# A fourth Strassen unit in the last gate pair of a decoder trunk layer

## The chip, the cores and the metric

One core of one Trainium2 chip. The metric is the device time of one execution in microseconds, the median over several runs. Engines are called PE or TensorE (matmul), PEld (its weight load), DVE or VectorE, ACT or ScalarE, POOL or GpSimd, and SP (SyncE, which issues the DMAs).

## The reference

One layer on 256 tokens of 2048 features, all in float32. A combined projection feeds a short convolution and a gated recurrence, two merge gates join them, `w_o` projects back into the residual, and then comes the part that this case is about:

```python
x = x + m @ w_o[i]
gate = jax.nn.sigmoid(rmsnorm(x, ple_norm_g[i]) @ w_ple_gate[i])     # 256 x 2048 by 2048 x 2048
x = x + gate * (p[i] @ w_ple_proj[i])
return rmsnorm(x, final_norm_g)
```

## The kernel before

**Tiling.** The tokens are two tiles of 128 (`t` = 0, 1). Weight columns come in groups of `CW` = 512, weight rows in chunks of 256 (two contractions of 128). A float32 product is made as three matmuls of 128 x 128 by 128 x 512: every operand is split into a high part (ScalarE, line 166, tiles `whi`, `xh`) and the rest (VectorE, line 167, `wlo`, `xl`), and high by high, high by rest and rest by high are summed in PSUM. So each weight tile goes from DRAM into `raw` (three buffers of 1 MB, filled from SP's queue, lines 119 to 131), is split, and is used. VectorE reads `raw` last, so its split is what lets the third load after it start.

**Strassen units.** Where two column groups share the left operand, a chunk can be done for both groups at once as a 2 x 2 by 2 x 2 block product (token tiles by contractions, contractions by groups). Plainly that is 8 block products; in Winograd's form of Strassen's scheme, 7. A unit costs vector work instead: the left operand's four sums (`forms`, lines 787 to 795, tiles `So0` and `So1` for the last pair), and four sums of the weights (`combine_weights`, lines 184, 187 and 188, made in place in `raw` and in a tile `t2`). Seven weight blocks of 128 x 512 are then split, as three tiles of 128 x 1024 and one of 128 x 512; a plain chunk of both groups has four, in two tiles of 128 x 1024. A program such as

```python
LATE = (0, 4), ("S", 0), (0, 6), ("S", 1), (2, 3), ("S", 2), (1, 4), (1, 6)
```

sets the order of a pair: `("S", c)` is a unit on chunk c; `(u, c)` with u = 0 or 1 is chunks c and c + 1 of group u alone; `(2, c)` is chunk c of both groups, plainly. Each entry is one load of 1 MB. The products of an entry are made in `pair_products` (line 1293), those of a plain group in `product` (line 1269).

**Banks.** PSUM has four banks under the tag `g` and four under `s`. A pair holds its four results (t, group) in `g` and the four products that several results share (numbers 1, 5, 6 and 7) in `s`. When they are complete, `sums` joins them: ScalarE copies product 1 out of its bank (line 868), and VectorE adds the others step by step (line 855). A tag's banks are given out in turn, so the next one asked for waits for the oldest to be read.

**The last 75 us.** First group 0 of `w_ple_gate`, plain. Then groups 1 and 2 as a pair by `LATE`. Then group 3 (`last_group`) in three passes over the same eight weight steps: all 512 columns for t = 0, then 256 and 256 for t = 1. Behind each finished gate half stand a sigmoid (ScalarE, line 1025), the product with the projection (VectorE, 1028), the sum into the residual `xs` (VectorE, 1029), its squares (ScalarE, 1030) and the gain (GpSimd, 1037). For the last group these are lines 1045, 1046, 1049 and 1053; lines 1062 to 1074 sum the squares, and the output is scaled (1087 to 1091) and stored.

**Order.** The program is written in the order of the weight steps; splits are issued some steps ahead of their products, and the rest of the vector work is written between them. Each engine then runs its own list in order, and waits on semaphores.

Of the kernel before, what the change touches and what calls it, by code (L numbers as in the profile page):

```python
# [23 lines left out]
CW = 512  # L24
# [19 lines left out]
INNER = (0, 4), ("S", 0), (0, 6), ("S", 1), (2, 3), ("S", 2), (1, 4), (1, 6)  # L44
FRONT = (0, 2), (0, 4), (0, 6), ("S", 0), (1, 2), ("S", 1), (1, 4), (1, 6)
OUT = (0, 4), ("S", 0), (1, 4), ("S", 1), (2, 3), ("S", 2), (0, 6), (1, 6)
LATE = (0, 4), ("S", 0), (0, 6), ("S", 1), (2, 3), ("S", 2), (1, 4), (1, 6)


PRM_GMIX, PRM_GPLE, PRM_GHG, PRM_LB, PRM_CONV = 0, 16, 32, 40, 48  # L50
# [5 lines left out]
def hybrid_kernel(ctx, tc, xT, x, pT, prm, gfin, masks, w_in, w_a, w_b, w_o, w_pg, w_pp, out):  # L56
# [28 lines left out]
    def nm(s):  # L85
        uid[0] += 1
        return f"{s}_{uid[0]}"
# [5 lines left out]
    def bank(tag):  # L93
        return ps.tile([P, CW], F32, tag=tag, bufs=4, name=nm(tag))
# [48 lines left out]
    def split(pos, c0=0, c1=2 * CW):  # L143
        part = part_of[pos]
        src = load(pos)[:, part % 2, :]
        if joint[pos]:

            src = load(pos)[:, part == 3, :]
            if part == 1:
                src, c1 = half[unit_of[pos]], CW  # L150

        pool, n = (pools["late"], 6) if (pos - state.get("late", len(steps))) % 10 < 6 and "late" in state else (wp, 4)
        places = [(pool, n, tag) for tag in ("whi", "wlo")]
        n = len(MORE[more(pos)])
        if pos % (4 + n) < n:
            places = [(pools[name], 1 + (tag == "X"), tag) for name, tag in MORE[more(pos)][pos % (4 + n)]]
        if pos not in parts:
            parts[pos] = tuple(
                pool.tile([P, 2 * CW << (tag[:3] == "yaT")], F32R, tag=tag, bufs=n, name=nm("w" + x))[:, : 2 * CW] for (pool, n, tag), x in zip(places, ("hi", "lo"))
            )  # L160
        hi, lo = parts[pos]
        s = slice(c0, c1)
        with ExitStack() as order:
            for i in (*(state["splits"] if more(pos) == "inner" or any(pos in at for at in tied) else ()),):
                order.enter_context(tc.issue_after(i))
            a = nc.scalar.activation(out=hi[:, s], in_=src[:, s], func=AF.Copy)  # L166
            v = nc.vector.tensor_tensor(  # L167
                out=lo[:, s], in0=src[:, s], in1=hi[:, s].bitcast(F32), op=ALU.subtract
            )
        state["splits"] = (a.ins, v.ins)  # L170
        if joint[pos] and part == 0:
            combine_weights(pos)
# [31 lines left out]
    groups += [("OO", 0, w_o, 0, "mT", OUT), ("O", 2, w_o, 2, "mT"), ("O", 3, w_o, 3, "mT")]  # L204
    groups += [("PG", 0, w_pg, 0, "x1T"), ("GP", 1, w_pg, 1, "x1T", LATE), ("PG", 3, w_pg, 3, "x1T")]
    steps = []
# [744 lines left out]
    def ep_o(j, psum):  # L951
# [18 lines left out]
        if j < 2:  # L970
# [6 lines left out]
            yield  # L977
            chunks = [c for u, c in LATE if u == "S" and c // 2 == j]
            r = x1.rearrange("p (u k t) -> p u k t", u=2, k=2)[:, : len(chunks)]
# [59 lines left out]
    def last_half(t, h, psum):  # L1039

        xs, pw, ss, n = state["x"], state["pw", 3], state["ss3"], CW // 2
        gt = t4()
        squares, gt = gt[:, : n + (t == 1 and h == 1)], gt[:, :n]
        d = xs[:, t, 3 * CW + h * n : 3 * CW + (h + 1) * n]
        nc.scalar.activation(out=gt, in_=psum, func=AF.Sigmoid, scale=state["rstd2"][:, t : t + 1])
        nc.vector.tensor_tensor(  # L1046
            out=gt, in0=gt, in1=pw[:, t * CW + h * n : t * CW + (h + 1) * n], op=ALU.mult
        )
        nc.vector.tensor_tensor(out=d, in0=d, in1=gt, op=ALU.add)
        if t == 1 and h == 1:  # L1050

            d = state["whole"][:, NT * D - n : NT * D + 1]
        nc.vector.scalar_tensor_tensor(
            out=squares, in0=d, scalar=1.0 / D, in1=d, op0=ALU.mult, op1=ALU.mult,
            accum_out=ss[:, t * 6 + 3 + h : t * 6 + 4 + h],
        )

    def sums_so_far(t):

        tot = state["tot3", t] = sc(1, "tot3", 2)  # L1060
        ss = state["ss3"]
        nc.vector.tensor_tensor(
            out=ss[:, t * 6 + 3 : t * 6 + 4], in0=ss[:, t * 6 + 3 : t * 6 + 4],
            in1=ss[:, t * 6 + 5 : t * 6 + 6], op=ALU.add,
        )
        nc.vector.tensor_reduce(
            out=tot, in_=ss[:, t * 6 : t * 6 + 4], axis=mybir.AxisListType.X, op=ALU.add
        )
        if t == 1:

            root = sc(1, "tot3", 2)
            nc.vector.tensor_scalar(out=tot, in0=tot, scalar1=float(D), scalar2=None, op0=ALU.mult)
            nc.gpsimd.tensor_tensor(out=root, in0=tot, in1=mhalf[:, :1], op=ALU.pow)
            nc.vector.tensor_tensor(out=state["more"], in0=tot, in1=root, op=ALU.mult)
# [29 lines left out]
    def ep_last(t, halves):  # L1104

        last_half(t, 0, halves[0])
        sums_so_far(t)
        last_half(t, 1, halves[1])
        last_norm(t)
        yield  # L1110
# [138 lines left out]
    def advance():  # L1249
        for e in list(active):  # L1250
            step(e)
# [12 lines left out]
    def product(psum, op, k, t, hi, lo, first, last, which=(0, 1, 2)):  # L1264

        oh, ol = (x[:, k, t * P : (t + 1) * P] for x in op)
        for n in which:
            a, b = ((oh, hi), (oh, lo), (ol, hi))[n]
            m = nc.tensor.matmul(psum, a, b, start=first and n == 0, stop=last and n == 2)  # L1269
            if late + 5 <= pos < late + 12:  # L1270
                tc.keep_in_program_order(m)
# [62 lines left out]
    for pos, (gi, c) in enumerate(steps[:last_group]):  # L1334
# [85 lines left out]
        for i in range(2):  # L1420
            k = 2 * c + i
            for c0, c1 in EARLY[0][:2] if pos == 0 and i == 0 else ((0, CW),):
                s = slice(i * CW + c0, i * CW + c1)
# [35 lines left out]

    nlast = len(steps) - last_group  # L1460
    for t, halves in ((0, (0, 1)), (1, (0,)), (1, (1,))):
        bk, n = bank("g"), CW // 2
        for c in range(nlast):
            if done < len(steps):
                split(done)
                done += 1
            hi, lo = parts[last_group + c]
            for i in range(2):
                k = 2 * c + i
                s = slice(i * CW + halves[0] * n, i * CW + (halves[-1] + 1) * n)  # L1470
                product(bk[:, : len(halves) * n], state["x1T"], k, t, hi[:, s], lo[:, s], k == 0, k == KT - 1)
            if c % 2:
                advance()
        if t == 0:
            active.append(ep_last(t, [bk[:, h * n : (h + 1) * n] for h in halves]))
        else:
            last_half(t, halves[0], bk[:, :n])
            if halves[0] == 0:
                sums_so_far(t)
# [76 lines left out]
```

## Time and profile before

| | |
|---|---|
| median of 3 runs | 807.52 us (807.15 to 807.83) |
| the profiled execution | 807.97 us, span 806.2 us, clock 0.997 |
| PE busy | 797.0 us, 99% of the span |
| DVE busy | 686.9 us, 85% |
| ACT busy | 494.1 us, 61% |
| POOL busy | 89.2 us, 11% |
| chain that ended last | PE 93%, DVE 3% |

A row of a timeline has the start in us from the first instruction, the duration in us, engine, line, operation, output <- inputs, shapes and a count of merged instructions; in brackets the time that the engine sat idle just before, and what released it. Durations overlap by the pipeline, so the cost of one in a row of equals is the distance of the starts.

### The profile page before, as it was taken

The page shows a single profiled execution, that of the slowest core. Times are in us where ns is not written, and L with a number is a line of the kernel's source. Part 1 is how long each engine was busy: PE and PEld are TensorE (multiplying, and loading weights), DVE is VectorE, ACT ScalarE, POOL GpSimd, SP SyncE. Part 2 cuts the span into 40 slices and gives each one's busy share as a digit, 9 for nine tenths or more (in the row PEclk, how much of TensorE's full clock was granted, in tenths as well). Part 3 has the DMA queues.
Part 4 walks back from the last instruction along what each step waited for, and adds up shares of the span by engine and source line. Part 5 has one row for each costly group of instructions (what it writes and reads, how often), then busy time and mean ns, then how long its engine had stood idle before and what let it go on. Part 6 is the DMA issues. An engine that isn't in the chain of part 4 may idle for free.

```text
span 806.2 us, 11109 instructions
## 1 busy us (share of the span) xinstructions
PE 797.0 (99%) x4168; PEld 662.5 (82%) x4169; DVE 686.9 (85%) x794; ACT 494.1 (61%) x666; POOL 89.2 (11%) x74
## 2 busy tenths in 40 slices
PE   9999999999999999999999999999999999999995
PEld 7888888888888888888888888888888888888885
DVE  6969897966778987978998998998998998879894
ACT  7867575575665665586674564564565556765652
POOL 0000145300000054300001000100100000002012
PEclk9999999999999999999999999999999999999998
DMA  9899855747776755668584775775875669987532
GB/s 344 308 322 314 275 169 205 242 167 231 251 262 197 257 179 202 209 206 261 187 310 159 220 277 168 249 260 184 263 274 196 209 240 350 368 268 258 222 120 104
DMA packets 50309, 191.20 MB, mean 237 GB/s; under 512 B 5712, under 2 KB 15184, under 8 KB 36304
## 3 DMA queue, kind: packets, MB, share of 16 engines
q1 hardware_dynamic: 50112, 190.24, 68.7%
q8 instruction: 32, 0.52, 0.3%
q10 hardware_dynamic: 144, 0.26, 0.1%
q14 instruction: 21, 0.17, 0.1%
HBM read 175.80 MB, written 14.68 MB: 236 GB/s over the span
## 4 chain that ended last, share of the span: by engine, by line
PE 93%; DVE 3%; issue 1%; ACT 1%; DMA 1%; POOL 0%; ACTq 0%; POOLq 0%; DVEq 0%
PE g L1269 49%; PE g L1293 30%; PE s L1293 8%; PE s L1269 3%; DVE wlo L167 1%; PE s L514 1%; DMA raw<-in_w_pg 1%; PE s L1142 1%; DVE t L855 0%; DVE t L1028 0%; ACT whi L166 0%; DVE t L1046 0%; DVE xs L1029 0%; PE s L647 0%; PE s L670 0%
## 5 line engine op out<-in xcount | busy, mean ns | idle before, releaser
L167 DVE TENSOR_TENSOR wlo<-raw,whi 128x1024 fp32r<-128x1024 f32 (+1 forms) x320 | 392.2, 1249 | 85.0 <-ACT whi L166 83.6
L166 ACT ACTIVATE whi<-raw 128x1024 fp32r<-128x1024 f32 (+1 forms) x320 | 326.3, 1047 | 167.4 <-PE g L1269 93.4
L1269 PE MATMUL g<-whi,xh 128*128 128x512 f32 (+1 forms) x464 | 177.5, 383 | 0.0
L1269 PE MATMUL g<-whi,xl 128*128 128x512 f32 (+1 forms) x464 | 177.2, 382 | 0.0
L1269 PE MATMUL g<-wlo,xh 128*128 128x512 f32 (+1 forms) x464 | 177.1, 382 | 0.0
L1293 PE MATMUL g<-wlo,xh 128*128 128x512 f32 x316 | 122.9, 389 | 0.0
L1293 PE MATMUL g<-whi,xl 128*128 128x512 f32 x316 | 122.9, 389 | 0.0
L1293 PE MATMUL g<-whi,xh 128*128 128x512 f32 x316 | 122.4, 389 | 0.0
L1269 PEld LDWEIGHTS g<-whi,xh 128*128 128x128 f32 x464 | 87.2, 188 | 17.2 <-ACT xh L313 0.4
L1269 PEld LDWEIGHTS g<-whi,xl 128*128 128x128 f32 x464 | 87.2, 188 | 17.1 <-DVE xl L314 0.2
L1269 PEld LDWEIGHTS g<-wlo,xh 128*128 128x128 f32 x464 | 87.2, 188 | 16.6
L166 ACT ACTIVATE whi<-t 128x512 fp32r<-128x512 f32 x25 | 15.8, 632 | 91.3 <-DVE t L187 86.7
L1293 PEld LDWEIGHTS g<-wlo,xh 128*128 128x128 f32 x316 | 59.3, 188 | 12.4
L1293 PEld LDWEIGHTS g<-whi,xh 128*128 128x128 f32 x316 | 59.3, 188 | 12.3
L1293 PEld LDWEIGHTS g<-whi,xl 128*128 128x128 f32 x316 | 59.3, 188 | 12.2
L184 DVE TENSOR_TENSOR raw<-raw 128x1024 f32<-128x1024 f32 x25 | 31.5, 1262 | 0.7
L937 POOL TENSOR_TENSOR t<-ga,gb 128x512 f32<-128x512 f32 x6 | 10.6, 1788 | 188.0 <-issue 118.1
L1269 PE MATMUL g<-whi,yaTh 128*128 128x512 f32 (+1 forms) x74 | 28.3, 389 | 0.0
L1269 PE MATMUL g<-whi,yaTl 128*128 128x512 f32 (+1 forms) x74 | 28.0, 384 | 0.0
L1269 PE MATMUL g<-wlo,yaTh 128*128 128x512 f32 (+1 forms) x74 | 27.9, 383 | 0.0
L1269 PE MATMUL g<-whi,ybTh 128*128 128x512 f32 x64 | 24.9, 389 | 0.0
L1269 PE MATMUL g<-wlo,ybTh 128*128 128x512 f32 x64 | 24.9, 389 | 0.0
(317 smaller groups left out, 1110.6 us busy)
## 6 DMA issues: line engine op xcount, KB each, us to landing
raw<-in_w_in SPq DMA_DIRECT2D x68, 1024.0 KB, 5.0
raw<-in_w_in SPq DMA_DIRECT2D x37, 512.0 KB, 5.3
raw<-in_w_o SPq DMA_DIRECT2D x12, 1024.0 KB, 5.6
raw<-in_w_pg SPq DMA_DIRECT2D x12, 1024.0 KB, 6.5
raw<-in_w_in SPq DMA_DIRECT2D x38, 256.0 KB, 5.6
turn<-t SPq DMA_DIRECT2D x72, 128.0 KB, 2.8
t<-turn SPq DMA_DIRECT2D x18, 512.0 KB, 5.2
raw<-in_w_a SPq DMA_DIRECT2D x8, 1024.0 KB, 5.6
```

The costliest lines, as they stand in the source:

```text
L166: a = nc.scalar.activation(out=hi[:, s], in_=src[:, s], func=AF.Copy)
L167: v = nc.vector.tensor_tensor(out=lo[:, s], in0=src[:, s], in1=hi[:, s].bitcast(F32), op=ALU.subtract)
L184: nc.vector.tensor_tensor(out=b[:, 0:4:3, :], in0=b[:, 0:3:2, :], in1=b[:, 3:4, :].to_broadcast([P, 2, CW]), op=ALU.subtract)
L514: nc.tensor.matmul(heads(bk)[r, h, c if at is None else slice(at, at + 32)], key(h)[:, r], query(h)[:, c], start=True, stop=True, tile_pos ...
L937: (nc.vector if j == 3 else nc.gpsimd).tensor_tensor(out=spread(m, t), in0=blocks(ga[:, s]), in1=blocks(gb[:, s]), op=ALU.add)
L1142: nc.tensor.matmul(wb[:m, :n], *ones, start=True, stop=True)
L1269: m = nc.tensor.matmul(psum, a, b, start=first and n == 0, stop=last and n == 2)
L1293: m = nc.tensor.matmul(banks[name], x, y[:, s], start=k == total[name] and i == 0, stop=k == 1 and i == 2)
```

## The change

The pair's program has a fourth unit, on chunk 3, in the place of the plain chunk of both groups, and the plain entry (1, 4) moves ahead of the third unit. The last group's first pass takes its bank from the tag `s`; its second and third take theirs from `g` as before.

```diff
-LATE = (0, 4), ("S", 0), (0, 6), ("S", 1), (2, 3), ("S", 2), (1, 4), (1, 6)
+LATE = (0, 4), ("S", 0), (0, 6), ("S", 1), (1, 4), ("S", 2), ("S", 3), (1, 6)
...
     nlast = len(steps) - last_group
     for t, halves in ((0, (0, 1)), (1, (0,)), (1, (1,))):
-        bk, n = bank("g"), CW // 2
+        bk, n = bank("g" if t else "s"), CW // 2
```

Units on chunks 2 and 3 take their forms from one tile, so `So1` has 1024 columns instead of 512. TensorE has 3 matmuls fewer, VectorE 5 instructions more, ScalarE 2.

On VectorE, behind the third unit's combination (before: `raw_6540` is the third unit, 6589 and 6611 are the plain entries (1, 4) and (1, 6), 6646 is the last group's first load):

```order
L167 TENSOR_TENSOR wlo_6628<-raw_6540,whi_6627 128x1024
L167 TENSOR_TENSOR wlo_6637<-raw_6589,whi_6636 128x1024
L167 TENSOR_TENSOR wlo_6649<-raw_6589,whi_6648 128x1024
L167 TENSOR_TENSOR wlo_6659<-raw_6611,whi_6658 128x1024
L167 TENSOR_TENSOR wlo_6677<-raw_6611,whi_6676 128x1024
L167 TENSOR_TENSOR wlo_6694<-raw_6646,whi_6693 128x1024
```

And now (`raw_6539` is the third unit, 6588 the fourth, 6612 the entry (1, 6), 6651 the last group's first load):

```order
L167 TENSOR_TENSOR wlo_6629<-raw_6539,whi_6628 128x1024
L167 TENSOR_TENSOR wlo_6638<-raw_6588,whi_6637 128x1024
L184 TENSOR_TENSOR raw_6588<-raw_6588 128x2x512
L187 TENSOR_TENSOR t_1194_6641<-raw_6588 128x512
L188 TENSOR_TENSOR raw_6588<-raw_6588,t_1194_6641 128x512
L167 TENSOR_TENSOR wlo_6681<-raw_6588,whi_6680 128x1024
L167 TENSOR_TENSOR wlo_6654<-t_1194_6641,whi_6653 128x512
L167 TENSOR_TENSOR wlo_6664<-raw_6588,whi_6663 128x1024
L167 TENSOR_TENSOR wlo_6697<-raw_6612,whi_6696 128x1024
L167 TENSOR_TENSOR wlo_6709<-raw_6612,whi_6708 128x1024
L167 TENSOR_TENSOR wlo_6716<-raw_6651,whi_6715 128x1024
```

The three rows of a combination and one and a half splits more stand ahead of the splits for the entry (1, 6) and for the last group.

Also on VectorE, around the last split of the program (before: `raw_6727` is the last load; `t_1208` and `t_1209` are the two gates of the pair):

```order
L1028 TENSOR_TENSOR t_1208_6712<-t_1208_6712,pw_6544 128x512
L167 TENSOR_TENSOR wlo_6770<-raw_6703,whi_6769 128x1024
L1029 TENSOR_TENSOR xs<-xs,t_1208_6712 128x512
L167 TENSOR_TENSOR wlo_6788<-raw_6727,whi_6787 128x1024
L167 TENSOR_TENSOR wlo_6804<-raw_6727,whi_6803 128x1024
L855 TENSOR_TENSOR t_1209_6713<-t_1209_6713,g_6561 128x512
L855 TENSOR_TENSOR t_1209_6713<-t_1209_6713,g_6683 128x512
L1028 TENSOR_TENSOR t_1209_6713<-t_1209_6713,pw_6634 128x512 x2
L1029 TENSOR_TENSOR xs<-xs,t_1209_6713 128x512 x2
```

And now (`raw_6747` is the last load, `t_1218` and `t_1219` are the gates):

```order
L167 TENSOR_TENSOR wlo_6784<-raw_6747,whi_6783 128x1024
L855 TENSOR_TENSOR t_1218_6756<-t_1219_6757,g_6482 128x512
L1028 TENSOR_TENSOR t_1218_6756<-t_1218_6756,pw_6543 128x512
L855 TENSOR_TENSOR t_1219_6757<-t_1219_6757,s_6549 128x1024
L1029 TENSOR_TENSOR xs<-xs,t_1218_6756 128x512
L1028 TENSOR_TENSOR t_1218_6756<-t_1218_6756,pw_6543 128x512
L167 TENSOR_TENSOR wlo_6812<-raw_6747,whi_6811 128x1024
L1029 TENSOR_TENSOR xs<-xs,t_1218_6756 128x512
L855 TENSOR_TENSOR t_1219_6757<-t_1219_6757,g_6560 128x512
L855 TENSOR_TENSOR t_1219_6757<-t_1219_6757,g_6670 128x512
L1028 TENSOR_TENSOR t_1219_6757<-t_1219_6757,pw_6635 128x512 x2
L1029 TENSOR_TENSOR xs<-xs,t_1219_6757 128x512 x2
```

The last split stood two behind the first gate's second L1029; it now stands ahead of it. The pair's later sums (L855) and the gate rows keep their order among themselves.

## The prediction

> **What bounds the kernel now.** I read the page first, then TensorE's own timeline, then VectorE (DVE) over the last 55 us, and last what releases VectorE there: ScalarE, GpSimd (POOL) and the weight loads.
>
> ```profile
> span 806.2 us, 11109 instructions
> PE 797.0 (99%) x4168; PEld 662.5 (82%) x4169; DVE 686.9 (85%) x794; ACT 494.1 (61%) x666; POOL 89.2 (11%) x74
> 734.00:776.00 42.00, 42.00 (x187) 34.76 (x186) 39.44 (x41) 26.46 (x33) 5.37 (x2) 1.00 0.59 213
> ```
>
> The third line is the view by stretches for the last gate pair (columns PE, PEld, DVE, ACT, POOL, clock, DMA share, GB/s). TensorE is busy for all of its 42.00 us at clock 1.00, but VectorE is busy for 39.44 of them. TensorE sets the pace and VectorE has 6% to spare: an edit that trades matmuls for vector work has to be read on both.
>
> ```profile
> 775.56 0.39 PE L1269 MATMUL g<-whi,xh 128*128 128x512 f32 x1
> 786.44 0.28 PE L1269 MATMUL g<-whi,xh 128*128 128x256 f32 x1
> 797.83 0.28 PE L1269 MATMUL g<-whi,xl 128*128 128x256 f32 x1
> 798.15 0.47 ACT L1045 ACTIVATE t<-g,r2r 128x256 f32<-128x256 f32 x1 [4.37 <-PE g L1269]
> 798.65 0.43 DVE L1046 TENSOR_TENSOR t<-t,pw 128x256 f32<-128x256 f32 x1 [2.03 <-ACT t L1045]
> 796.46 0.16 DVE L1074 TENSOR_TENSOR xs<-tot,tot 128x1 f32<-128x1 f32 x1 [0.73 <-POOL tot L1073]
> ```
>
> The first two rows are the first matmul of the last group and the first of its second pass. Between them are 48 matmuls: (786.44 - 775.56)/48 = 0.2267 us each (the 0.39 is latency, they overlap). The last three rows are the end. After the last matmul ScalarE evicts at 798.15, and VectorE, which finished its earlier work (L1074) at 796.62, has waited 2.03 us for that. So the end is TensorE's, and **VectorE's slack there is 2.03 us**: work that arrives later than that at L1074 takes the end over.
>
> How tight VectorE is before that:
>
> ```profile
> 764.69 2.36 DVE L167 TENSOR_TENSOR wlo<-raw,whi 128x1024 fp32r<-128x1024 f32 x2 [1.50 <-ACT whi L166]
> 775.56 0.69 DVE L1028 TENSOR_TENSOR t<-t,pw 128x512 f32<-128x512 f32 x1 [0.18 <-ACT t L1025]
> 777.30 1.78 DVE L1029 TENSOR_TENSOR xs<-xs,t 128x512 f32<-128x512 f32 x1
> 780.14 2.31 DVE L167 TENSOR_TENSOR wlo<-raw,whi 128x1024 fp32r<-128x1024 f32 x1
> 782.37 1.27 DVE L855 TENSOR_TENSOR t<-t,g 128x512 f32<-128x512 f32 x2
> 783.84 1.31 DVE L1028 TENSOR_TENSOR t<-t,pw 128x512 f32<-128x512 f32 x2 [0.19 <-ACT t L1025]
> 787.51 2.08 DVE L1046 TENSOR_TENSOR t<-t,pw 128x256 f32<-128x256 f32 x2 [1.16 <-ACT t L1045]
> 786.41 0.62 ACT L1030 ACTIVATE t<-xs 128x512 f32<-128x512 f32 x1
> 787.03 0.82 ACT L1045 ACTIVATE t<-g,r2r 128x256 f32<-128x256 f32 x2
> ```
>
> From 758 to 782 VectorE waits 1.50 and 0.18 us and no more. The split at 780.14 is the last of the kernel and ends at 782.45; TensorE asks for it in the eighth step of the last group's first pass, at 775.56 + 42 x 0.2267 + 0.23 = 785.31. That is a lead of 2.9 us. Then the second gate's sums (782.37), products (783.84) and adds follow, ScalarE squares them (786.41), and only then, at 787.03, evicts the last group's first sums, though TensorE had them by about 786.6. From there on each step waits for the one before up to L1074. So what delays VectorE at 782 arrives whole at 796.62.
>
> **TensorE: the gain.** A plain 256-row chunk for both gates costs 8 products of 3 matmuls, a Strassen unit 7: 24 against 21, so 3 x 0.2267 = 0.68 us less. In the order the program stands in, PE has 3 rows fewer. That is the whole of the gain, and the last matmul would start at 797.15. It is under 0.2% of the time (1.6 us), about what a measurement of this kernel can tell from no change.
>
> **VectorE: the price.** The unit's weights have to be combined and split in 3.5 tiles instead of 2.
>
> ```profile
> 745.35 0.69 DVE L188 TENSOR_TENSOR raw<-raw,t 128x512 f32<-128x512 f32 x1
> 745.96 1.22 DVE L167 TENSOR_TENSOR wlo<-raw,whi 128x1024 fp32r<-128x1024 f32 x1
> 747.10 0.69 DVE L167 TENSOR_TENSOR wlo<-t,whi 128x512 fp32r<-128x512 f32 x1
> 747.70 4.62 DVE L167 TENSOR_TENSOR wlo<-raw,whi 128x1024 fp32r<-128x1024 f32 x4
> 752.36 1.23 DVE L184 TENSOR_TENSOR raw<-raw 128x1024 f32<-128x1024 f32 x1
> 753.62 0.69 DVE L187 TENSOR_TENSOR t<-raw 128x512 f32<-128x512 f32 x1
> 754.34 0.69 DVE L188 TENSOR_TENSOR raw<-raw,t 128x512 f32<-128x512 f32 x1
> 758.58 3.49 DVE L167 TENSOR_TENSOR wlo<-raw,whi 128x1024 fp32r<-128x1024 f32 x3
> ```
>
> From start to start: L184 1.26, L187 0.72, L188 0.61 (745.35 to 745.96), a full split 1.14, the half split 0.60. A unit is 2.59 + 3 x 1.14 + 0.60 = 6.61, and 6.72 with the 0.11 by which the first L184 starts late. A plain pair of splits takes 2.27. **The extra is 4.45 us** on VectorE. ScalarE gets about 1.5 splits more; it has 16 us free in this stretch, so that costs nothing.
>
> I walk VectorE from 758.58 (the last row above), the first split behind the third unit; up to there its rows are the same as before. The new unit's first split goes at 758.58, L184 at 759.8, L187 761.1, L188 761.8, splits at 762.4, 763.6 and 764.2, the last plain pair at 765.3, the first load of the last group at 767.6, and VectorE is through with that at 769.9. TensorE, which would begin the last group at 775.56 - 0.68 = 774.88, asks for the new unit's third part 36 matmuls earlier, at 766.7, and it is ready at 765.4: no stall.
>
> Then the weight loads. A load goes out when the third buffer before it is split:
>
> ```profile
> 758.68 0.33 SPq L131 DMA_DIRECT2D raw<-in_w_pg  x1
> 760.95 2.60 SPq L131 DMA_DIRECT2D raw<-in_w_pg  x2
> 763.60 2.01 ACT L166 ACTIVATE whi<-raw 128x1024 fp32r<-128x1024 f32 x2 [2.59 <-DMA raw<-in_w_pg]
> 767.08 2.01 ACT L166 ACTIVATE whi<-raw 128x1024 fp32r<-128x1024 f32 x2 [0.99 <-DMA raw<-in_w_pg]
> ```
>
> The first of a run takes 763.60 - 758.68 = 4.9 us until ScalarE has it, the second 767.08 - 760.95 = 6.1. The last group's second load uses the buffer of the new unit, free at 765.4 instead of 760.9. It is the first of its run, 6.8 us after the one before, so I take 4.9: ScalarE at 770.4, VectorE 1.09 later (763.60 to 764.69) at 771.5, after a wait of 1.66. That stands where the 1.50 was; with 6.1 it would be 2.9.
>
> GpSimd's gain products come after ScalarE's squares, one for each half of a gate:
>
> ```profile
> 777.17 1.37 POOL L1037 TENSOR_TENSOR xs<-xs,gfin_t 128x512 f32<-128x512 f32 x1 [32.40 <-ACT t L1030]
> 779.92 1.45 POOL L1037 TENSOR_TENSOR xs<-xs,gfin_t 128x512 f32<-128x512 f32 x1 [1.38 <-ACT t L1030]
> ```
>
> Beside them the VectorE rows at 777.30 (1.78, else 0.69) and 780.14 (2.31, else 1.22) are longer by 1.09 each, and end just after GpSimd's: they are held. In the new order the last split stands ahead of the second L1029, at 782.7 in my walk, before GpSimd starts at about 783.1. So it goes free and ends at 783.95; TensorE asks at 784.6, a lead of 0.7 instead of 2.9. The L1029 behind it is held for 1.1, and the products behind the second gate's sums for 0.75 (GpSimd 786.55 to 787.9, products ready at 787.15): 1.85 against 2.18 before. The Trainium skill, "GPSIMD Engine Reference", section "Key points", says that GpSimd contends with vector instructions that have two SBUF inputs. By it the sums (L855, one input in PSUM) run free, and the trace agrees for the two-SBUF rows; no run here shows an L855 beside GpSimd. If those were held too, the price would be some 0.3 us more.
>
> **The sum.** VectorE's delay at L1028 and so at L1074: 4.45 + (1.66 - 1.50) - 0.18 + (1.85 - 2.18) = 4.1 us. Slack 2.03. The end comes **2.07 us later**, and the 0.68 us on TensorE are not seen. Profiled time 807.97 becomes 810.0. The median shown is 807.52, 0.45 below the profiled execution, so I forecast 809.6. If GpSimd's second hold doesn't happen the delay is 3.35 (+1.3); if the load takes 6.1 it is 5.3 (+3.3). A little looser: +0.9 to +3.3, 808.4 to 810.8.
>
> The Trainium skill, "DMA: Bandwidth & Descriptors", section "Anatomy of one DMA", gives 2.0 us and bytes/436e3 for a transfer from GpSimd's queue: an estimate of 4.4 us for 1 MB, and a sum of +1.6. These come from SP's queue and the trace has 4.9 at best, so I keep that.
>
> **Edits that cost nothing.** The second pair of forms has twice the width: four operations and a split on VectorE at 700 to 704, about 0.14 us more for each of the four (0.28 at 128 wide, 0.69 at 512) and 0.53 for the split (0.69 against 1.22), 1.1 us in all.
>
> ```profile
> 700.73 0.28 DVE L787 SCALAR_TENSOR_TENSOR t<-t 128x128 f32<-128x128 f32 x1
> 711.75 1.28 DVE L855 TENSOR_TENSOR xs<-xs,g 128x512 f32<-128x512 f32 x2
> 711.96 1.06 ACT L166 ACTIVATE whi<-raw 128x1024 fp32r<-128x1024 f32 x1 [1.38 <-PE g L1269]
> 714.82 1.14 ACT L957 ACTIVATE t<-xs 128x512 f32<-128x512 f32 x2
> 728.44 0.19 PEld L1269 LDWEIGHTS g<-whi,xh 128*128 128x128 f32 x1 [0.40 <-ACT xh L313]
> ```
>
> ScalarE waits until 711.96 for TensorE and then reaches L957 at 714.82 whatever VectorE did, and VectorE's adds ahead of L957 (711.75 before, at most 712.9 now) are done by 714.2. That cover matters, because L957 starts the chain by which TensorE waits at 728.44: if it is gone, up to 1.1 us come in whole. Taking the last group's first bank from the other four costs nothing: ScalarE copies the first sum out of it at about 773, and TensorE writes it at 774.9. In the old bank the release would be VectorE's sum at 774.4.
>
> **Rivals.** First, the other side: VectorE's tail has room that I don't see, and the cover holds. It needs a delay at L1074 under 2.03. If GpSimd held nothing, 4.45 + 0.16 - 0.18 - 2.18 = 2.25; with a load 0.3 us sooner as well it is under. Then the end is TensorE's again, down to the full 0.68: 806.8 to 808.0. Against it: every gain product in this stretch is seen holding a VectorE row. For it: the order of two engines at a lock can fall either way. Chance 0.22. Second, late weights: the second load takes 6.1 or the third and fourth crowd it, the last split ends after 784.6 and TensorE stops as well. VectorE's delay is then 5.3 or more: 810.8 to 812. Chance 0.08. Third, the forms cut into the chain at 728, which adds 0.3 to 1.1 to the main case: 809.9 to 810.7. Chance 0.05. That the change doesn't do what it says is excluded: the order has the 3 matmuls fewer and the fourth combination.
>
> **The numbers.** Main case 0.65, of which 0.48 lies above +1.6 us. Slower by over 0.2%: 0.48 + 0.08 + 0.05 = 0.61. Within 0.2%: 0.17 + 0.20 = 0.37. Faster by over 0.2%: 0.02, since more than the 0.68 would need something that no row shows. The range takes the full gain in, 806.8, and ends with the main case at 810.9; it leaves the late weights out.
>
> **What would show it.** Right: TensorE 0.2267 us a matmul without a gap up to the last group, the last split 1.5 us later than before, L1074 at about 800.7 and the last L1046 right behind it, its wait for ScalarE gone. Wrong: L1046 still waiting for L1045 (then the first rival, and the span is 0.7 shorter), or TensorE idle in the last group (the second), or a longer wait at 728 (the third).

## The result, and the profile after

The change takes 808.84 us (median of 22 executions, 807.67 to 810.50) against 807.79 us for the kernel before (22 executions beside it): ratio 1.0014, 95% interval 1.0007 to 1.0020. It is slower by 1.05 us. Its profiled execution took 809.69 us, 1.72 more than the 807.97 of before.

The page of the change (second part) and its view by stretches, over the last gate pair and the last group:

```profile
span 807.9 us, 11117 instructions
PE 795.5 (98%) x4165; PEld 661.3 (82%) x4166; DVE 691.5 (86%) x799; ACT 496.1 (61%) x668; POOL 89.6 (11%) x74
734.00:776.00 42.00, 42.00 (x187) 34.75 (x187) 39.55 (x41) 25.37 (x32) 5.37 (x2) 1.00 0.59 213
776.00:798.00 22.00, 21.64 (x141) 19.72 (x139) 19.44 (x32) 10.12 (x20) 6.63 (x5) 1.00 0.11 37
```

TensorE is still without a gap through the pair and busy for 1.5 us less in all; VectorE has 4.6 us more. The end, in the timelines of the change:

```profile
765.61 2.60 SPq L131 DMA_DIRECT2D raw<-in_w_pg  x2
770.49 2.01 ACT L166 ACTIVATE whi<-raw 128x1024 fp32r<-128x1024 f32 x2 [2.76 <-DMA raw<-in_w_pg]
728.64 0.19 PEld L1269 LDWEIGHTS g<-whi,xh 128*128 128x128 f32 x1 [0.89 <-ACT xh L313]
797.36 0.28 PE L1269 MATMUL g<-whi,xl 128*128 128x256 f32 x1
764.36 5.76 DVE L167 TENSOR_TENSOR wlo<-raw,whi 128x1024 fp32r<-128x1024 f32 x5
771.59 2.36 DVE L167 TENSOR_TENSOR wlo<-raw,whi 128x1024 fp32r<-128x1024 f32 x2 [1.46 <-ACT whi L166]
782.83 1.22 DVE L167 TENSOR_TENSOR wlo<-raw,whi 128x1024 fp32r<-128x1024 f32 x1
783.97 1.78 DVE L1029 TENSOR_TENSOR xs<-xs,t 128x512 f32<-128x512 f32 x1
785.67 1.27 DVE L855 TENSOR_TENSOR t<-t,g 128x512 f32<-128x512 f32 x2
787.15 1.88 DVE L1028 TENSOR_TENSOR t<-t,pw 128x512 f32<-128x512 f32 x2 [0.21 <-ACT t L1025]
783.15 2.05 POOL L1037 TENSOR_TENSOR xs<-xs,gfin_t 128x512 f32<-128x512 f32 x1 [38.17 <-ACT t L1030]
786.58 1.29 POOL L1037 TENSOR_TENSOR xs<-xs,gfin_t 128x512 f32<-128x512 f32 x1 [1.38 <-ACT t L1030]
800.34 0.16 DVE L1074 TENSOR_TENSOR xs<-tot,tot 128x1 f32<-128x1 f32 x1 [0.73 <-POOL tot L1073]
800.42 0.42 DVE L1046 TENSOR_TENSOR t<-t,pw 128x256 f32<-128x256 f32 x1
```

The last L1046 has no bracket any more: the 2.03 us for which it waited on ScalarE are gone, and it comes straight behind L1074. TensorE's last matmul is 0.47 earlier (797.83 to 797.36), and that buys nothing, because L1074 is 3.88 later (796.46 to 800.34).

The row at 728.64 explains why it is 0.47 and not 0.68. This weight load, which stands behind the chain at 728 that the prediction names, starts 0.20 later than before (728.44). From there to the last matmul TensorE takes 68.72 us where it took 69.39: 0.67 less, the three matmuls. The same 0.20 is in the 3.88: counted from that load, L1074 is 3.68 later and the end 1.57.

That start at 728 turned out to move between 728.1 and 729.4 from one profile to the next, in kernels of both kinds and whatever was changed behind it. So the profiles are best compared from there. Each row below is one kernel. "From 728" is the start of that load; "to last matmul" and "to L1046" count from it; "wait" is that of the last L1046 for ScalarE. A zero there says that VectorE sets the end. The last two columns come from all executions, against the kernel before on the same chip; difference and ratio are two estimates of the same thing, and differ by up to 0.07%, nearly as much as the 0.68 us (0.08%) that is looked for.

| kernel | from 728 | to last matmul | to L1046 | wait | median against before, us | ratio (95%) |
|---|---|---|---|---|---|---|
| before | 728.44 | 69.39 | 70.21 | 2.03 | | |
| the change | 728.64 | 68.72 | 71.78 | 0 | +1.05 | 1.0014 (1.0007 to 1.0020) |
| e1, old bank | 728.62 | 68.71 | 72.06 | 0 | +0.94 | 1.0007 (0.9998 to 1.0016) |
| e2, no combining | 729.19 | 68.73 | 69.55 | 1.03 | -0.05 | 0.9998 (0.9989 to 1.0007) |
| e3, no gain products | 729.36 | 68.73 | 69.55 | 0.67 | -0.50 | 0.9996 (0.9987 to 1.0005) |
| e4, before + 4 splits | 728.64 | 70.52 | 71.91 | 0 | -0.33 | 1.0003 (0.9994 to 1.0012) |
| e9, before + 8 splits | 728.64 | 74.01 | 75.39 | 0 | +4.76 | 1.0057 (1.0044 to 1.0070) |
| e7, evictions ahead | 729.18 | 68.96 | 70.60 | 0 | +0.10 | 1.0004 (0.9995 to 1.0012) |
| e10, early load | 728.92 | 68.73 | 69.55 | 0.28 | -0.40 | 0.9990 (0.9981 to 0.9999) |
| e11, both | 728.81 | 68.70 | 69.53 | 1.46 | -0.60 | 0.9992 (0.9983 to 1.0001) |
| e12, before + early load | 728.48 | 69.41 | 70.23 | 2.88 | -0.06 | 0.9998 (0.9989 to 1.0007) |
| e13, before + both | 729.21 | 69.41 | 70.23 | 2.32 | -0.18 | 0.9999 (0.9990 to 1.0008) |
| e14, both again | 728.08 | 68.73 | 69.55 | 1.45 | -0.84 | 0.9990 (0.9981 to 0.9999) |
| e15, early load again | 729.41 | 68.73 | 69.56 | 0.28 | -0.65 | 0.9996 (0.9987 to 1.0004) |

### The profile page after: what moved, and what is told of

The parts are those of the page before. It is cut to its first block, busy times and chain, and to the rows that moved or that the text cites. A ratio compares the mean times of both kernels' runs of the same rounds, so it can differ in the third digit from the quotient of the medians.

```text
span 807.9 us, 11117 instructions
## 1 busy us (share of the span) xinstructions
PE 795.5 (98%) x4165; PEld 661.3 (82%) x4166; DVE 691.5 (86%) x799; ACT 496.1 (61%) x668; POOL 89.6 (11%) x74
## 4 chain that ended last, share of the span: by engine, by line
PE 91%; DVE 3%; DMA 2%; ACT 1%; issue 1%; SPq 0%; POOL 0%; ACTq 0%; POOLq 0%
PE g L1269 47%; PE g L1293 30%; PE s L1293 8%; PE s L1269 3%; DVE wlo L167 1%; PE s L514 1%; DMA raw<-in_w_pg 1%; DMA t<-turn 1%; ACT whi L166 1%; DMA turn<-t 1%; DMA raw<-in_w_pp 1%; DVE t L1028 0%; DVE xs L1029 0%; DVE t L1046 0%; DVE t L855 0%
## 5 line engine op out<-in xcount | busy, mean ns | idle before, releaser
L1269 PE MATMUL g<-whi,xh 128*128 128x512 f32 (+1 forms) x448 | 171.3, 383 | 0.5 <-ACT xh L313 0.5
L1269 PE MATMUL g<-whi,xl 128*128 128x512 f32 (+1 forms) x448 | 171.0, 382 | 0.0
L1269 PE MATMUL g<-wlo,xh 128*128 128x512 f32 (+1 forms) x448 | 170.9, 382 | 0.0
L1293 PE MATMUL g<-wlo,xh 128*128 128x512 f32 x310 | 120.6, 389 | 0.0
L1293 PE MATMUL g<-whi,xl 128*128 128x512 f32 x310 | 120.6, 389 | 0.0
L1293 PE MATMUL g<-whi,xh 128*128 128x512 f32 x310 | 120.1, 389 | 0.0
L1269 PEld LDWEIGHTS g<-whi,xh 128*128 128x128 f32 x448 | 84.2, 188 | 17.1 <-ACT xh L313 0.9
L1269 PEld LDWEIGHTS g<-whi,xl 128*128 128x128 f32 x448 | 84.2, 188 | 16.4 <-DVE xl L314 0.2
L1269 PEld LDWEIGHTS g<-wlo,xh 128*128 128x128 f32 x448 | 84.2, 188 | 16.1
L1293 PEld LDWEIGHTS g<-wlo,xh 128*128 128x128 f32 x310 | 58.2, 188 | 12.1
L1293 PEld LDWEIGHTS g<-whi,xl 128*128 128x128 f32 x310 | 58.2, 188 | 12.1
L1293 PEld LDWEIGHTS g<-whi,xh 128*128 128x128 f32 x310 | 58.2, 188 | 12.0
```

Of the source, the lines that this page charges most:

```text
L1293: m = nc.tensor.matmul(banks[name], x, y[:, s], start=k == total[name] and i == 0, stop=k == 1 and i == 2)
```

## The experiments

### Which half of the change costs (e1, e2, e3)

The change with the last group's first sums in the old bank again:

```diff
-        bk, n = bank("g" if t else "s"), CW // 2
+        bk, n = bank("g"), CW // 2
```

> The change with its second half undone: the last group's first pass takes its bank from g again. Theory (the vector tail sets the end): in the profile of the change VectorE's sum has read that bank at 774.5 and TensorE's first matmul of the last group comes at 775.1, so nothing waits and the time is that of the change, 0.6 to 1.8 us over before. Rival (the bank is what holds TensorE): TensorE starts the last group up to 1 us later and the time is up to 1 us more than the change's.

808.87 us, as the change. The bank makes no difference that these runs can tell from noise; the loss stands without it, so it comes with the new program of the pair.

The change without the fourth unit's combination (its seven products are made from uncombined weights, so the chunk's part of both gates comes out wrong):

```diff
+            if pos == fourth:
+                half[unit_of[pos]] = b[:, 2, :]
+                return
```

> The change without the weight combination of the fourth unit (L184, L187, L188, 2.59 us of VectorE; so the unit multiplies the plain weights). Its splits, loads and matmuls stay. Theory: L1074 comes 3.88 - 2.59 = 1.3 us later than before, inside the slack of 2.03, so TensorE sets the end again and its gain shows: 0.4 to 0.7 us under before, with the last L1046 waiting for L1045 again, some 0.3 us. Rival (the loads or the longer program, not VectorE's time): still 0.5 to 1.5 us over before.

807.88 us, as before. The expected gain of 0.4 to 0.7 us does not show in the median, and the interval of the ratio (down to 0.9989) does not exclude it. Its timelines:

```profile
729.19 0.19 PEld L1273 LDWEIGHTS g<-whi,xh 128*128 128x128 f32 x1 [1.02 <-ACT xh L317]
780.23 1.29 DVE L1033 TENSOR_TENSOR xs<-xs,t 128x512 f32<-128x512 f32 x2
781.44 1.22 DVE L167 TENSOR_TENSOR wlo<-raw,whi 128x1024 fp32r<-128x1024 f32 x1
784.05 2.17 DVE L1032 TENSOR_TENSOR t<-t,pw 128x512 f32<-128x512 f32 x2 [0.19 <-ACT t L1029]
797.55 0.16 DVE L1078 TENSOR_TENSOR xs<-tot,tot 128x1 f32<-128x1 f32 x1 [0.73 <-POOL tot L1077]
798.74 0.43 DVE L1050 TENSOR_TENSOR t<-t,pw 128x256 f32<-128x256 f32 x1 [1.03 <-ACT t L1049]
```

L1078 is here what L1074 is in the change: 797.55 instead of 800.34, and 3.34 sooner when both are counted from 728. The wait for ScalarE is back. Of the 3.34, 2.59 are the three operations (from start to start). The rest, 0.75, comes from another order of VectorE's rows: both L1033 (the change's L1029) of the first gate stand ahead of the last split here, so none of them is held, and only the products L1032 lose about 0.9. With the 2.59 alone the wait for ScalarE would still be about 0.3 us, so by these figures the combination by itself is enough to decide who sets the end. From 728 the end is 0.66 sooner than before (69.55 against 70.21), but this profiled execution started 0.75 later there, so its span is that of before.

The change without GpSimd's four gain products for the pair's two gates (groups 1 and 2), so that these columns lack their gain:

```diff
+            if j == 0:
                 nc.gpsimd.tensor_tensor(out=d, in0=d, in1=state["gfin"][:, j * CW : (j + 1) * CW], op=ALU.mult)
```

> The change without the four gain products on GpSimd behind the pair (L1037 for its two gates is left out, so these columns lack the final gain). Theory: VectorE's rows that are held beside them (783.97, 787.15 and 791.39 in the profile of the change, 1.1, 0.6 and 1.2 us too long) are free, L1074 comes some 2.9 us sooner than in the change, 1.0 later than before, and TensorE sets the end: 0.4 to 0.7 us under before. Rival (GpSimd holds nothing, its rows only stand beside slow ones): as the change, 0.6 to 1.8 us over before.

807.43 us. Its VectorE timeline:

```profile
784.65 0.69 DVE L1029 TENSOR_TENSOR xs<-xs,t 128x512 f32<-128x512 f32 x1
786.75 1.30 DVE L1028 TENSOR_TENSOR t<-t,pw 128x512 f32<-128x512 f32 x2 [0.22 <-ACT t L1025]
790.42 0.79 DVE L1047 TENSOR_TENSOR t<-t,pw 128x256 f32<-128x256 f32 x2 [1.17 <-ACT t L1046]
798.91 0.42 DVE L1047 TENSOR_TENSOR t<-t,pw 128x256 f32<-128x256 f32 x1 [0.67 <-ACT t L1046]
```

The three rows that GpSimd lengthened in the change, 1.78, 1.88 and 2.08, are 0.69, 1.30 and 0.79: 1.09, 0.58 and 1.29 of holding, 2.96 in all. From 728 its L1075 (the change's L1074) is 2.98 sooner than in the change, which is these holds. Without them TensorE sets the end.

### How much room VectorE has (e4, e9)

The kernel before with splits of the last pair made a second time, four and eight of them, 1.14 us each:

```diff
+            if pos in again:
+                nc.vector.tensor_tensor(out=lo[:, s], in0=src[:, s], in1=hi[:, s].bitcast(F32), op=ALU.subtract)
```

> The kernel before, with the four vector splits of the entries (1, 4) and (1, 6) made twice: 4 x 1.14 = 4.55 us more on VectorE and nothing else, about the 4.45 of the fourth unit. Theory: L1074 comes about 4 us later, 2.03 are slack, and the time is 1.0 to 2.3 us over before, as with the change, although TensorE's work, the loads and the banks are those of before. Rival (the price of the change lies in its loads or its matmul order): within 0.3 us of before.

> The kernel before, with the four splits of the entries (1, 4) and (1, 6) made three times: 8 x 1.14 = 9.1 us more on VectorE. It measures the slack of executions without the profiler. If it is the 2.03 that the profile shows, the median is 6 to 7 us over before. If ordinary executions have 2 us more room than the profiled one (the four repeated splits cost 1.9 us in their profile and about nothing in the median), it is 4 to 5 over, and the profile 6 to 7.

Timelines of the one with four:

```profile
765.59 2.35 DVE L171 TENSOR_TENSOR wlo<-raw,whi 128x1024 fp32r<-128x1024 f32 x2
777.86 1.06 ACT L166 ACTIVATE whi<-raw 128x1024 fp32r<-128x1024 f32 x1 [1.96 <-DMA raw<-in_w_pg]
779.56 0.69 DVE L1033 TENSOR_TENSOR t<-t,pw 128x512 f32<-128x512 f32 x1 [1.03 <-ACT t L1030]
786.50 0.50 PE L1274 MATMUL g<-wlo,xh 128*128 128x512 f32 x1 [0.58 <-DVE wlo L167]
800.47 0.16 DVE L1079 TENSOR_TENSOR xs<-tot,tot 128x1 f32<-128x1 f32 x1 [0.73 <-POOL tot L1078]
800.55 0.42 DVE L1051 TENSOR_TENSOR t<-t,pw 128x256 f32<-128x256 f32 x1
```

and of the one with eight:

```profile
784.95 0.19 PEld L1275 LDWEIGHTS g<-wlo,xh 128*128 128x128 f32 x1 [1.41 <-DVE wlo L167]
803.96 0.16 DVE L1080 TENSOR_TENSOR xs<-tot,tot 128x1 f32<-128x1 f32 x1 [0.73 <-POOL tot L1079]
```

With 4.56 us more work L1079 is 4.01 later, and this one profile costs 1.9 us. TensorE is held too: it waits for the last split at 786.50, and its last matmul comes 70.52 us from 728 instead of 69.39 (74.01 with eight). VectorE still sets the end, but these two kernels are not a pure case of it.

The median costs nothing: 807.60 us, seven of the eleven executions between 807.2 and 807.7 and the profiled one, 809.88, the longest. The expectation of a loss missed in the median. With 9.12 us more the profile's chain ends 7.50 later, and the median (of five executions) rises by 4.76, as expected; the profile takes 5.41 more than that of before, where 6 to 7 was expected. So the first half of the added work cost about nothing in the median and the second about 5. Most ordinary executions with four splits had more room on VectorE than the profiled one; with eight, profile and median differ by 0.65 us only.

One wait of the profile with four splits can be named. The last load goes out at 770.25 and ScalarE has it at 777.86, 7.6 us after (6.8 before, 767.08 to 773.85), and by that VectorE waits 1.03 us at 779.56. Without this wait L1079 would be about 3.0 us later instead of 4.01. Whether ordinary executions are spared it isn't shown, since only profiled executions leave rows, and by itself it isn't enough.

### Giving VectorE its room back (e7, e10, e11)

The last group's evictions ahead of the second gate's squares on ScalarE, and the small product L1074 behind the last L1046 on VectorE (a part of the edit, shortened):

```diff
+        gts = [last_gate(t, half) for half in halves]
+        for i in range(NT):
+            square(2, i, ...)
-        last_half(t, 0, halves[0])
+        last_half(t, 0, halves[0], gts[0])
+        gain_product(2, 0)
```

> The change with the end of its vector chain shortened and nothing taken away: the last group's first evictions (L1045 of the change) are put ahead of the squares of the second gate on ScalarE, and the last half's first two vector operations ahead of the root column (L1074), so that its wait for GpSimd is filled. Theory (the chain of VectorE, ScalarE and GpSimd sets the end of the change): it ends 1.2 + 0.5 us sooner, so 1.0 to 2.0 us less than the change, 0 to 0.6 under before, about where TensorE sets the end. Rival (the change is slower for a reason ahead of that chain, such as TensorE's wait at 728): as the change, 0.6 to 1.6 over before.

807.87 us, about 1.0 under the change and 0.1 over before, where 0 to 0.6 under before was expected. VectorE's timeline has why not more:

```profile
790.72 0.75 DVE L1061 TENSOR_TENSOR t<-t,pw 128x256 f32<-128x256 f32 x2
791.39 2.94 DVE L1064 TENSOR_TENSOR xs<-xs,t 128x256 f32<-128x256 f32 x2
799.78 0.42 DVE L1061 TENSOR_TENSOR t<-t,pw 128x256 f32<-128x256 f32 x1
```

The wait of 1.17 ahead of the first L1061 is gone and its hold with it (0.75 instead of 2.08), but GpSimd's gain products now meet the next row, L1064: 2.94 instead of 0.75. A hold that is moved isn't removed.

The last group's second load sent early, as two 512 KB transfers into the tiles of the first forms, which are free by then (shortened):

```diff
+        if unit_of[pos] not in loaded and pos == last_group + 2:
+            two = [pools["tmp3"].tile([P, 2 * CW], F32R, tag="So0" + x, bufs=1, ...).bitcast(F32) for x in "hl"]
+            for i in range(2):
+                nc.sync.dma_start(out=two[i], in_=w[g, :, c + i, :])
```

> The change, with the last group's second load put into the tiles of the first pair of forms, which are free by then, so that it doesn't wait for the fourth unit's buffer. Theory: VectorE's wait of 1.46 us at 771.6 is gone, in the profile L1074 comes some 1.4 sooner and the end 0.2 to 0.6 over before; the median is within 0.5 of before. Rival (in executions without the profiler the loads land early anyway, and the wait is only the profiled one's): the profile falls by 1.2 to 1.5 and the median stays at 0.6 to 1.5 over before.

807.37 us, 0.40 under before and some 1.5 under the change. Its timelines:

```profile
764.64 8.03 DVE L179 TENSOR_TENSOR wlo<-raw,whi 128x1024 fp32r<-128x1024 f32 x7
781.33 1.21 DVE L179 TENSOR_TENSOR wlo<-raw,whi 128x1024 fp32r<-128x1024 f32 x1
782.46 0.68 DVE L1041 TENSOR_TENSOR xs<-xs,t 128x512 f32<-128x512 f32 x1
783.06 1.27 DVE L867 TENSOR_TENSOR t<-t,g 128x512 f32<-128x512 f32 x2
781.63 2.67 POOL L1049 TENSOR_TENSOR xs<-xs,gfin_t 128x512 f32<-128x512 f32 x1 [36.38 <-ACT t L1042]
798.03 0.16 DVE L1086 TENSOR_TENSOR xs<-tot,tot 128x1 f32<-128x1 f32 x1 [0.73 <-POOL tot L1085]
798.47 0.42 DVE L1058 TENSOR_TENSOR t<-t,pw 128x256 f32<-128x256 f32 x1 [0.28 <-ACT t L1057]
```

The 1.46 us ahead of the load's splits are gone: seven splits in one run. Besides, a hold changed sides. GpSimd's first gain product comes 0.30 us after the last split has begun, and it waits through that split and through L1041 behind it (2.67 instead of 1.37), while L1041 runs in 0.68. In the change the rows stand in the same order and GpSimd comes 0.32 after the split has begun, yet there it got in behind the split, and L1029, the same step as L1041, took 1.78. Why it fell the other way isn't shown; e7, which has no early load, also has the 2.67 (784.52). L1074's step is at 798.03, 2.31 sooner than in the change, and 2.59 from 728: about the 1.46 of the load and the 1.10 of the hold. TensorE sets the end again, by 0.28 us. With the 1.46 alone L1074's step would be at 70.2 from 728 and VectorE would still set the end of this profile, so the early load owes its success in part to the hold.

Both together:

> Both edits of the last two kernels on the change. Theory: VectorE's last work before the final eviction ends 1 us or more before TensorE does, TensorE sets the end, and the 0.68 us of the fewer matmuls show: 0.4 to 0.8 us under before. Rival: no better than before, because something else takes the end over.

807.17 us, 0.60 under before. The wait for ScalarE in front of the last addition is 1.46 us now.

### Is it the fourth unit that gains? (e12 to e15)

The early load alone, and both edits, in the kernel before, with its three units; and the two four-unit kernels once more, beside them.

> The kernel before (three units) with the second load of the last group sent early into the tiles of the first forms, as in the run of the change with that load. Theory (TensorE sets the end of the kernel before, VectorE has 2.03 us to spare there, so an earlier load only adds to the spare time): within 0.2 us of the kernel before, ratio 0.9998 to 1.0003, and the last L1046's form waits about 3.5 us for ScalarE (2.03 + the 1.50 of the load). Rival (the early load itself helps, by some other way than VectorE's tail, and the fourth unit has no part in the gain): 0.4 to 0.8 us under before, as the change with the early load had it.

> The kernel before (three units) with the early load and with the last group's evictions put ahead of the second gate's squares. Theory: TensorE sets the end, so within 0.2 us of the kernel before; the control for the change with both. Rival (the two edits gain alone): 0.4 to 0.8 us under before.

> The change with the early load and the evictions put ahead, as run before, in more runs beside its own control. Theory: the fourth unit is worth its 0.68 us on TensorE less what the wait at 728 us happens to take, so 0.4 to 0.7 us under before and under the control with three units. Rival (the fourth unit is worth nothing even with room on VectorE): equal to the control within 0.2 us.

> The change with the early load alone, as run before, in more runs. Theory: TensorE sets the end by a little, 0.4 to 0.8 us under before and under the early load with three units. Rival: equal to the early load with three units within 0.2 us.

The timelines of e13 (three units) and of e14 (four), with both edits in each:

```profile
729.21 0.19 PEld L1302 LDWEIGHTS g<-whi,xh 128*128 128x128 f32 x1 [1.71 <-ACT xh L325]
799.44 0.42 DVE L1073 TENSOR_TENSOR t<-t,pw 128x256 f32<-128x256 f32 x1 [2.32 <-ACT t L1064]
```

```profile
728.08 0.19 PEld L1302 LDWEIGHTS g<-whi,xh 128*128 128x128 f32 x1
728.60 0.19 PEld L1302 LDWEIGHTS g<-whi,xl 128*128 128x128 f32 x1 [0.15 <-DVE xl L326]
796.81 0.28 PE L1302 MATMUL g<-whi,xl 128*128 128x256 f32 x1
797.63 0.42 DVE L1073 TENSOR_TENSOR t<-t,pw 128x256 f32<-128x256 f32 x1 [1.45 <-ACT t L1064]
```

With three units neither edit moves the time: 807.81 and 807.69 us against 807.87. VectorE only waits longer for ScalarE: 2.88 us at the end of e12, where 3.5 was expected, because a part of the wait moved to the last group's first products (2.49 instead of 1.16):

```profile
787.20 0.91 DVE L1058 TENSOR_TENSOR t<-t,pw 128x256 f32<-128x256 f32 x2 [2.49 <-ACT t L1057]
```

With four units the medians are 807.03 and 807.22. Four against three, both edits in: 0.66 us less (e14 against e13); the early load alone in: 0.59 less (e15 against e12). The intervals against before are 0.9981 to 0.9999 (e14) and 0.9987 to 1.0004 (e15). All executions with both edits and four units (e11, e14) against all with three units (e12, e13), which are on one chip, give 0.9993, with 0.9989 to 0.9997 as the middle 95% when medians are drawn anew from these executions. So where VectorE does not set the end, the fourth unit is worth about the 0.68 us of its three matmuls, with that spread around it. In the profile of e14 the chain at 728 hardly holds TensorE (no wait at 728.08, 0.15 behind it), and its span is 805.1.

## Why the prediction was right, and where it was not

**TensorE's gain, 0.68 us.** Right. Every four-unit kernel needs 68.70 to 68.73 us from 728 to its last matmul (e7 alone 68.96, where TensorE waits for the last split), where those with three units and no added work need 69.39 to 69.41.

**VectorE's delay at L1074, 4.1 us.** Right in the profile: 3.88, of which 0.20 is the later start at 728 and 3.68 the change. By its terms: the last split was put at 782.7 and started at 782.83; the load's wait was put at 1.66 and measured 1.46; the two holds at 1.85 and measured 1.67 (1.10 at L1029 and 0.57 at L1028). The load went out at 765.61 and ScalarE had it at 770.49, 4.9 us after, as taken from the rows of before. The estimate of 4.4 us by the formula of the Trainium skill's "DMA: Bandwidth & Descriptors", section "Anatomy of one DMA", which is for GpSimd's queue, gave a sum of +1.6. That came near the 1.77 measured, and nearer still to the 1.57 from 728, but by luck: the transfer itself took the 4.9 that the rows say, and it was the shorter wait on VectorE and the shorter holds that brought the end there.

**The sums L855 aren't held.** Right, and now seen: in the early-load kernel both (L867 there: 1.27 from 783.06) run at their normal length beside GpSimd's product, which ends at 784.30. The Trainium skill's "GPSIMD Engine Reference", section "Key points", names vector instructions with two SBUF inputs as those that contend with GpSimd, and the trace agrees: these sums have one. The Trainium skill's "SBUF — State Buffer", section "SBUF: two separate sides", has an exclusive lock, held for the whole instruction by whoever starts first. The trace agrees that the other engine waits, with L1029 held to 1.78 in the change and GpSimd held to 2.67 in the early-load kernel; which of the two goes on behind the split differs between these kernels.

**The forms cut into the chain at 728.** That rival is out. The cover held:

```profile
711.81 1.28 DVE L855 TENSOR_TENSOR xs<-xs,g 128x512 f32<-128x512 f32 x2
714.53 1.14 ACT L957 ACTIVATE t<-xs 128x512 f32<-128x512 f32 x2
726.80 1.25 DVE L358 STREAM_TRANSPOSE t<-t 128x1024 f32<-128x1024 f32 x1 [0.88 <-DMA t<-turn]
```

VectorE's adds stand at 711.81 in the change (711.75 before) because VectorE's wait ahead of them shrank from 1.57 to 0.46 us, and ScalarE reaches L957 at 714.53 (714.82 before). So the wider forms delayed neither. The wait at 728 moved from 0.40 to 0.89 in the two profiles, but 0.77 stands in a kernel with the old forms (e4), and 1.71 in another (e13). It varies by itself by more than the gain.

**The end, +2.07 us, and 809.6.** Here a step failed. In the profile the end came 1.77 later (1.57 from 728), near the forecast. The median rose by 1.05. The step that failed is the last one: "the median shown is 807.52, 0.45 below the profiled execution, so I forecast 809.6". It took the slack and the waits of one execution as those of all, and the distance of 0.45 as the same for a kernel with another bound. (Against the median of the 22 executions of before, 807.79, its own distance is 0.18.) For the change the distance is 0.85, for e1 1.05, for e4 2.28, for e7 1.30, for e9 0.85: all of them kernels in which VectorE sets the end. For those in which TensorE does, it is 0.45 on average (-0.14 to 1.09 in e2, e3 and e10 to e15). So the sign was right and the time in the range, but "slower by over 0.2%" was given 0.61, and the measured 0.14% is on the near side of that bound: the term was sized at nearly twice what ordinary executions pay. That VectorE's waits for loads are shorter in ordinary executions would fit e4, and e9 only for a small part, since its profile and its median rise by 5.41 and 4.76. It stays argued; no run here shows rows of an unprofiled execution, so the cause of the 0.5 us between 1.57 and 1.05 is open.

**The rival "VectorE's tail has room".** It named the right quantity, and in the change the room was not there: GpSimd's holds came as forecast. Its point, a delay under 2.03 us, is where e2, e3 and e10 land. Its thought that the order of the two engines can fall either way came true in e10, though not in the change.

## What to carry to other kernels

Where one engine sets the pace and another is at 94%, an edit that takes matmuls away and adds vector work has to pay on the second engine's own chain to the end. Work out its slack at the last meeting point before the gain; here 0.68 us of TensorE time needed 4.45 of VectorE with 2.03 to spare, and only with one late load and one hold out of the way did it pay. And where an expected difference is under a few tenths of a percent, one profile says which engine set the end of that one execution, but not by how much, and in e4 not even what the median does: compare profiles from the last common event, and take the size from medians.

## What the runs showed of the hardware

GpSimd's operation also waits for VectorE, so a long row of GpSimd can be waiting and not work. In the change and in e1 GpSimd came 0.32 us after a split had begun, took 2.05 us, got in behind the split, and the next VectorE row with two SBUF inputs lost 1.10. In e7, e10, e11, e14 and e15 the same rows stood in the same order, GpSimd came 0.30 to 0.32 us after the split had begun, and it waited through the next row as well (2.67 us for an operation that takes 1.37 alone); VectorE lost nothing there. This is the row of e7:

```profile
784.52 2.67 POOL L1048 TENSOR_TENSOR xs<-xs,gfin_t 128x512 f32<-128x512 f32 x1 [39.02 <-ACT t L1041]
```

In e12 it waited through four VectorE rows that followed each other without a gap (4.94 us from 776.17). So neither the order of the rows nor the moment at which GpSimd comes tells which engine loses. What decides isn't shown, and a forecast has to carry both cases, as the prediction's first rival did.

The wait at 728, where TensorE waits for ScalarE's copy of the normalised rows, starts the next stage anywhere from 728.1 to 729.4 us in thirteen profiles besides before's. That is twice as wide as the gain that was looked for. ScalarE's L957, where this chain begins, starts at 714.3 to 715.1 us, so most of the spread arises behind it. In the change two DMA transfers (out to `turn` and back, 4.60 and 5.14 us) lie in that stretch. What makes the stretch vary was not tried.
